# A decoder step on one core: transfers of the opening in a new order, four transposes in another bank, a copy and a store placed anew

## The chip, the cores and the metric

The kernel runs on one core of a Trainium2 chip. The metric is the time of one execution on the device in microseconds, lower is better. Engines are called by their names: TensorE (PE in the profile, its weight loads PEld), VectorE (DVE), ScalarE (ACT), GpSimd (POOL), SyncE (SP). DMAs are issued by an engine's sequencer (SPq, ACTq) and run beside the engines.

## The reference, cut to what matters

One layer of a decoder for 512 prompt tokens and 8 x 8 sample tokens, 576 in all, with model width 1024:

```
h   = x @ w_in                    # [u | v | q | k | v_attn | gate_A | gate_B]
A   = gelu(u) * spatial mix of LN(gelu(v)), in chunks of 128 positions
B   = sliding-window attention (window 128, 16 heads, 4 key heads), with a sink
      per head and a relative position bias: rel_bias[bucket(distance)]
m   = (sigmoid(gate_A) * (A @ w_pa) + sigmoid(gate_B) * (B @ w_pb)) @ w_o
x   = LN1(alpha * x + m)
x   = LN2(alpha * x + (silu(x @ w_gate) * (x @ w_up)) @ w_down)
```

Results are x for both groups, the new key and value windows, and the normalised v of the sample tokens.

## The kernel before, in words

**Numbers.** All is float32. Each operand of a large product is split in two: ScalarE casts it to the format `fp32r` (hi), VectorE subtracts that from the source (lo). `split` (lines 113 to 115) does this, so line 114 is always a cast on ScalarE and line 115 a subtraction on VectorE. A product is then three matmuls: hi by hi, hi by lo, lo by hi.

**Stages.** All weights lie in one array, `wall`, of units of 128 x 1024 (512 KB). SyncE fetches them in the order of use into three buffers (`fetch`, line 117); a unit is fetched when the split of an earlier one has freed its buffer. The stages are: the opening, which makes the first key tile and the first query tile; the other projections with the attention between them; the gMLP; merge; output projection; FFN; and the down projection with the last layer norm. From the opening on, TensorE goes from one stage into the next.

**The opening** (`projections_and_attention`, from line 715). Ten dummy products on zeros (`warm_up`, line 389) stand first. The 1024 input rows are cut in 8 chunks of 128. `load_x` (line 397) asks for the tokens of chunk k (`xT[:, k]`, 128 x 576) and for the first weight unit in pieces: weights 0:256 (chunk 0), tokens 0, weights 256:512, tokens 1, weights 512:1024, two small tables for the position bias (`bias_lookup`, line 418), tokens 2 and 3 in one transfer, weight unit 1, tokens 4 and 5, tokens 6 and 7, weight unit 2. Chunk k needs its tokens split and a 128 x 256 piece of weights split; it is then twelve matmuls of 288 columns into two tiles, `ps0_0` (keys) and `ps0_1` (queries): for each half of the tokens and each tile, hi by hi, hi by lo, lo by hi. After chunk 1 stands one product of the bias tables (`bias_products`, line 431), whose result VectorE copies into rows (lines 439, 440). `bias_tables` (line 442) writes these rows to DRAM 128 times (`circ`) and reads them back with a stride (`Bsel`); the first attention scores add them (line 574).

In this part a planner of the framework sets the order of each engine's instructions, by what it expects to be ready. Code under `manual_schedule()` (the pairs of merge and FFN, lines 998, 1099 and 1226) keeps the order in which it is written. `issue_after` holds what stands under it behind a given instruction of the same engine.

**After the opening.** The next tile (`psq`, the second query tile, from weight unit 2) starts on TensorE, then the value projection (`psav`, units 3 and 4). ScalarE and VectorE meanwhile empty the two tiles: `evac_k` (line 463) makes four casts of the keys on ScalarE (line 470), four subtractions on VectorE (line 475), and last a copy of the newest 192 key columns to `kraw` on ScalarE (line 478). `evac_q` (line 480) does the queries (lines 490 to 500). The second key tile, `psk`, is emptied in the same way later. A tile of PSUM is used again when all of its readers are done; there are three such tiles of two banks (`PS`, line 104) and two single banks (`bank`, line 107).

**The sample's attention.** `sample_scores` makes the weights S of the eight sample sequences. In the next PSUM pool, of eight single banks, `sample_turn` (line 675) transposes S in two groups of four (line 685), copies each out (line 686), and transposes the weights of the new tokens (line 688). The banks of the new pool lie where the old pool's tiles lay, so its first ones wait until the last gate tile, `psg`, has been copied out (line 815).

**The end.** `last_norm` (line 1337) normalises the last 128 rows in three pieces of columns: c0 (416) and c1 (416) by VectorE, c (192) by ScalarE and GpSimd. c0 is stored from ScalarE's queue, c1 from SyncE's (line 1353), c from SyncE's after c1 (line 1355).

Of the kernel before, what the change touches and what calls it, by code (L numbers as in the profile page):

```python
# [18 lines left out]
P = 128  # L19
D = 1024  # L20
KC = D // P
# [55 lines left out]
class Builder:  # L77
# [311 lines left out]
    def warm_up(self):  # L389

        z = self.C([512], mybir.dt.bfloat16, "zero")
        self.nc.vector.memset(z[:], 0.0)
        ps = self.bank("warm")
        for _ in range(10):
            self.mm(ps, z[:, :P], z[:], True, True)

    def load_x(self):
        nc, xT = self.nc, self.I["xT"]
        r = [self.C([2, NT], F32, f"xraw{i}") for i in range(4)]
        self.xraw = [r[k // 2][:, k % 2] for k in range(KC)]  # L400
        raw = self.praw.tile([P, 1024], F32, tag="raw", name="raw0")
        self.raws.append(raw)
        for c0, c1, k in ((0, 256, 0), (256, 512, 1), (512, 1024, None)):
            nc.sync.dma_start(out=raw[:, c0:c1], in_=self.I["wall"][0][:, c0:c1])
            if k is not None:
                nc.sync.dma_start(out=r[0][:, k], in_=xT[:, k])
        self.bias_lookup()
        nc.sync.dma_start(out=r[1][:], in_=xT[:, 2:4])
        self.fetch(1)
        nc.sync.dma_start(out=r[2][:], in_=xT[:, 4:6])  # L410
        nc.sync.dma_start(out=r[3][:], in_=xT[:, 6:8])
        self.fetch(2)

    def xact(self, k):
        return self.X[:, k, :NT], self.X[:, k, NT:]
# [23 lines left out]
        nc.vector.tensor_copy(out=self.rows, in_=o[:, :W].unsqueeze(1).to_broadcast([P, 4, W]))  # L439
        nc.vector.tensor_copy(out=self.rows_s, in_=o[:, W:NBIAS])  # L440

    def bias_tables(self):

        nc = self.nc
        cd = self.pd.tile([H, W, W], F32, name="circ")
        nc.sync.dma_start(
            out=cd.rearrange("h (m a r) i -> (h m) a r i", m=8, a=4),
            in_=self.rows.unsqueeze(1).to_broadcast([P, 4, 4, W]))
        self.Bsel = [self.C([8, P], F32, f"Bsel{i}") for i in range(2)]
        for i in range(2):  # L450
            src = bass.AP(cd.tensor, cd.offset + 8 * i * W * W, [[W - 1, P], [W * W, 8], [1, P]])
            nc.sync.dma_start(out=self.Bsel[i][:], in_=src)
# [10 lines left out]
    def evac_k(self, ps, c):  # L463
        nc = self.nc
        self.kt += [self.C([2, NT], F32R, f"kt{2 * c + i}") for i in range(2)]
        f = lambda a: a.rearrange("p (b c) -> p b c", b=2)
        for i in range(2):
            s = slice(64 * i, 64 * i + 64)
            for o in range(2):
                nc.scalar.copy(out=f(self.kt[2 * c + i][64 * o : 64 * o + 64, 0]), in_=ps[s, :, :HB])  # L470
        for i in range(2):
            t = self.kt[2 * c + i]
            s = slice(64 * i, 64 * i + 64)
            for o in range(2):
                nc.vector.tensor_tensor(
                    out=f(t[64 * o : 64 * o + 64, 1]), in0=ps[s, :, :HB], in1=f(t[s, 0]).bitcast(F32),
                    op=ALU.subtract)
        nc.scalar.copy(out=self.kraw[:, c, :], in_=ps[:, 1, HB - 192 : HB])  # L478

    def evac_q(self, ps, c):  # L480
        nc = self.nc
# [190 lines left out]
            out=S[:], in0=S[:], in1=rec.unsqueeze(2).to_broadcast([P, DB, SK]), op=ALU.mult)  # L672
        return S

    def sample_turn(self, S):
        nc = self.nc
        f32c = lambda s, n: self.C(s, F32, n)
        pnew = self.SG("pnew")
        nc.vector.tensor_copy(
            out=pnew[:, :NS].rearrange("p (b j) -> p b j", b=DB), in_=S[:, :, W:])  # L680
        pT = f32c([DB, P], "spT")
        for c in range(2):
            ps = self.bank(f"pst{c}")
            for b in range(4):
                nc.tensor.transpose(ps[:, P * b : P * b + P], S[:, 4 * c + b, :W], self.ident[:])
            self.turned = nc.scalar.copy(out=pT[:, 4 * c : 4 * c + 4].rearrange("p b q -> p (b q)"), in_=ps)
        ps2 = self.bank("pst2")
        nc.tensor.transpose(ps2[:NS, :P], pnew[:, :NS], self.ident[:])
        pN = f32c([DB, P], "spN")
        nc.vector.tensor_tensor(  # L690
            out=pN[:NS], in0=ps2[:NS, :P].unsqueeze(1).to_broadcast([NS, DB, P]),
            in1=self.bmask[:NS].unsqueeze(2).to_broadcast([NS, DB, P]), op=ALU.mult)
        return pT, pN
# [21 lines left out]
    def projections_and_attention(self):  # L715
        nc = self.nc
        self.X = self.px.tile([P, KC, 2 * NT], F32R, tag="x", name="X")
        self.XS = self.C([KC, P], F32R, "XS")
        misc = self.misc = self.C([1152], F32, "misc")
        self.kraw = misc[:, :384].rearrange("p (c t) -> p c t", c=2)  # L720
        self.Z = self.C([G, 4, 32], F32, "Z")
        self.kt, self.qs, self.u, self.T = [], {}, [], []
        self.warm_up()
        self.load_x()
        self.small_tables()
        tiles = [self.PS(f"ps0_{c}") for c in range(2)]
        for k in range(KC):
            if k % 4 == 0:
                u = self.unit(4, parts=4, ahead=0)
            for t0, t1 in ((0, HB), (HB, NT)) if k == 0 else ((0, NT),):  # L730
                self.split(self.X[:, k, t0:t1], self.X[:, k, NT + t0 : NT + t1], self.xraw[k][:, t0:t1])
            xh, xl = self.xact(k)
            for c in range(2):
                wh, wl = (w[:, k % 4, P * c : P * c + P] for w in u)
                for b in range(2):
                    s = slice(b * HB, (b + 1) * HB)
                    o = tiles[c][:, b, :HB]
                    self.mm(o, wh, xh[:, s], k == 0, False)
                    self.mm(o, wh, xl[:, s], False, False)
                    self.mm(o, wl, xh[:, s], False, k == KC - 1)  # L740
            if k == 1:
                self.bias_products()
        self.convert(2)
        self.bias_tables()
        self.convert(4)
        self.evac_k(tiles[0], 0)
        self.evac_q(tiles[1], 0)
        self.first_read = self.evacuated
        self.run(self.column_tile("q", 1))
        with self.tc.issue_after(self.placed.ins):  # L750
            nc.vector.tensor_copy(out=self.XS[:, :, :NS], in_=self.X[:, :, NP:NT].bitcast(F32))
            nc.vector.tensor_copy(out=self.XS[:, :, NS:], in_=self.X[:, :, NT + NP :].bitcast(F32))
        self.yB = []
        blocks = [(g, n) for g in range(G) for n in range(NB)]
        fills = FILLS
        probs = []
        self.values(lambda: probs.append(self.attention_scores(*blocks[len(probs)])))
        self.sample_bias()
        self.run(self.column_tile("q", 2))
        for i, (g, n) in enumerate(blocks):  # L760
            if n == 0:
                self.yB.append(self.C([2, NT], F32, f"yB{g}"))
            turned = self.attention_turn(g, n, probs[i])
            if i:
                with self.tc.issue_after(self.last_turned.ins):
                    self.attention_values(*waiting)
            if i + 2 < len(blocks):
                probs.append(self.attention_scores(*blocks[i + 2]))
                if i + 4 == len(blocks):
                    with self.tc.issue_after(self.selected.ins):  # L770
                        kc, vc = self.sample_keys()
            elif i + 1 < len(blocks):
                S = self.sample_scores(kc)
            if i:
                with self.tc.issue_after(self.lower.ins), self.tc.issue_after(self.shifted.ins):
                    self.run(fill)
            waiting = g, n, turned
            before_last = i + 2 == len(blocks)
            fill = self.column_tile(*fills[i], ahead=1 + before_last)
            next(fill, None)  # L780
            if i + 1 == len(blocks):
                with self.tc.issue_after(self.last_mm.ins):
                    self.attention_values(*waiting)
            next(fill, None)
            if i + 3 == len(blocks):
                self.run(fill)
        self.run(fill)
        self.sample = S, vc

    def sample_first(self):  # L790
        S, vc = self.sample
        turned = self.sample_turn(S)
        self.sample_rest = lambda: self.sample_values(vc, *turned)

    def run(self, gen):
# [541 lines left out]
    def last_norm(self, st, z, g, b, dst):  # L1337
# [12 lines left out]
        for k, queue in ((c0, nc.scalar), (c1, nc.sync)):  # L1350
            nc.vector.scalar_tensor_tensor(
                out=z[:, k], in0=z[:, k], scalar=r[:], in1=b[:, k], op0=ALU.mult, op1=ALU.add)
            sent = queue.dma_start(out=dst[:, k], in_=z[:, k])
        with self.tc.issue_after(sent.ins):
            nc.sync.dma_start(out=dst[:, c], in_=z[:, c])


def _weights(w_in, w_pa, w_pb, w_o, w_gate, w_up, w_down):
# [107 lines left out]
```

## Time and profile before

| what | us |
|---|---|
| runs shown, median (lowest to highest of 3) | 887.53 (887.2 to 889.0) |
| the profiled execution, its own time | 887.54 |
| its span, first to last instruction | 885.8 |
| TensorE busy in the span | 873.7 |
| VectorE / ScalarE / GpSimd busy | 630.7 / 405.8 / 195.5 |
| span from 0 to 12: TensorE busy | 9.52 |

Times in the profile are microseconds from the first instruction. A row of the timeline gives start, length, engine, line of the kernel, operation, tile written and tile read, shapes and count (rows that follow each other closely are merged), and in brackets how long the engine stood idle before it and what released it. `DMA` as a releaser is the landing of a transfer. A row of the table by stretches gives for each engine the busy time and in brackets the number of instructions, then the granted clock of TensorE as a share of full, the DMA engines' busy share, and GB/s moved. The chain of waits follows the work that ended last back from the end.

### The profile page before, as it was taken

The page shows a single profiled execution, that of the slowest core. Times are in us where ns is not written, and L with a number is a line of the kernel's source. Part 1 is how long each engine was busy: PE and PEld are TensorE (multiplying, and loading weights), DVE is VectorE, ACT ScalarE, POOL GpSimd, SP SyncE. Part 2 cuts the span into 40 slices and gives each one's busy share as a digit, 9 for nine tenths or more (in the row PEclk, how much of TensorE's full clock was granted, in tenths as well). Part 3 has the DMA queues.
Part 4 walks back from the last instruction along what each step waited for, and adds up shares of the span by engine and source line. Part 5 has one row for each costly group of instructions (what it writes and reads, how often), then busy time and mean ns, then how long its engine had stood idle before and what let it go on. Part 6 is the DMA issues. An engine that isn't in the chain of part 4 may idle for free.

```text
span 885.8 us, 14732 instructions
## 1 busy us (share of the span) xinstructions
PE 873.7 (99%) x5911; PEld 821.0 (93%) x5911; DVE 630.7 (71%) x934; ACT 405.8 (46%) x769; POOL 195.5 (22%) x205
## 2 busy tenths in 40 slices
PE   8999999999999999999999999999999999999996
PEld 7999999988899999999988999999999998888885
DVE  6778897646789789768777777777777789224237
ACT  6567566566355356334422544444444457111110
POOL 3013324242332113133302222222222210000003
PEclk9999999999999999999999999999999999999999
DMA  8431225144023224324450023233323325323202
GB/s 301 137 115 53 69 72 146 60 170 162 24 81 110 94 75 161 108 105 154 165 201 18 1 72 96 96 96 95 95 97 96 95 96 190 96 72 95 72 1 107
DMA packets 31168, 91.85 MB, mean 104 GB/s; under 512 B 3963, under 2 KB 9372, under 8 KB 31068
## 3 DMA queue, kind: packets, MB, share of 16 engines
q1 hardware_dynamic: 30908, 88.74, 30.6%
q10 hardware_dynamic: 192, 2.18, 0.6%
q8 instruction: 46, 0.75, 0.3%
q14 instruction: 22, 0.18, 0.1%
HBM read 86.77 MB, written 6.10 MB: 105 GB/s over the span
## 4 chain that ended last, share of the span: by engine, by line
PE 92%; DVE 4%; ACT 1%; issue 1%; DMA 1%; SPq 0%; POOL 0%; DVEq 0%; ACTq 0%; POOLq 0%
PE d L295 16%; PE xf L295 14%; PE zf L295 7%; PE acc_v L295 6%; PE acc_o L295 6%; PE pspa L295 6%; PE xg L295 5%; PE psu L295 5%; PE yf L295 4%; PE psq L295 3%; PE ffn L295 3%; PE zg L295 3%; PE xp L295 2%; PE psav L295 2%; PE psg L295 1%; PE yg L295 1%
## 5 line engine op out<-in xcount | busy, mean ns | idle before, releaser
L115 DVE TENSOR_TENSOR lo<-raw,hi 128x1024 fp32r<-128x1024 f32 (+1 forms) x78 | 89.8, 1159 | 96.7 <-ACT hi L114 96.3
L115 DVE TENSOR_TENSOR glo<-raw,ghi 128x1024 fp32r<-128x1024 f32 (+1 forms) x93 | 100.8, 1087 | 55.3 <-ACT ghi L114 55.3
L295 PE MATMUL d<-hi,h 128*128 128x512 f32 (+1 forms) x440 | 128.0, 368 | 0.0
L114 ACT CAST hi<-raw 128x1024 fp32r<-128x1024 f32 (+1 forms) x78 | 75.7, 984 | 105.9 <-PE d L295 82.6
L114 ACT CAST ghi<-raw 128x1024 fp32r<-128x1024 f32 (+1 forms) x93 | 83.4, 900 | 58.8 <-DVE raw L177 54.2
L295 PEld LDWEIGHTS d<-hi,h 128*128 128x128 f32 x440 | 79.8, 188 | 13.8
L295 PE MATMUL d<-lo,h 128*128 128x512 f32 (+1 forms) x242 | 89.6, 370 | 0.0
L177 POOL TENSOR_TENSOR raw<-raw,t 128x512 f32<-128x512 f32 x31 | 40.7, 1314 | 198.4 <-DVE glo L115 170.3
L177 POOL TENSOR_TENSOR t<-raw,raw 128x512 f32<-128x512 f32 x31 | 42.1, 1358 | 117.5 <-DVE raw L177 117.5
L295 PE MATMUL xf<-x1T,ghi 128*128 128x288 f32 x320 | 64.9, 295 | 0.0
L115 DVE TENSOR_TENSOR glo<-t,ghi 128x1024 fp32r<-128x1024 f32 x31 | 64.5, 2082 | 0.0
L295 PEld LDWEIGHTS d<-lo,h 128*128 128x128 f32 x242 | 45.6, 188 | 7.8
L295 PEld LDWEIGHTS xf<-x1T,ghi 128*128 128x128 f32 x320 | 51.3, 188 | 0.2 <-DVE u L226 0.2
L325 POOL TENSOR_SCALAR lnr<-lnmv 128x1 f32<-128x1 f32 (+1 forms) x15 | 12.3, 821 | 168.8 <-DVE lnmv L343 165.5
L608 POOL TENSOR_SCALAR_AFFINE_SELECT pc<-pt 128x512 fp32r<-128x512 f32 x24 | 23.1, 962 | 110.9 <-ACT pt L114 109.2
L295 PE MATMUL xf<-x1T,glo 128*128 128x288 f32 x160 | 47.1, 294 | 0.0
L295 PE MATMUL acc_o<-hi,m 128*128 128x512 f32 x144 | 46.4, 391 | 0.0
L295 PE MATMUL pspa<-yA,hi 128*128 128x288 f32 x256 | 44.6, 294 | 0.3 <-DVE yA L115 0.3
L295 PE MATMUL psu<-X,hi 128*128 128x288 f32 x256 | 44.1, 294 | 0.0
L584 ACT ACTIVATE work<-work,att 128x128 f32<-128x128 f32 x64 | 25.0, 392 | 40.9 <-DVE att L581 40.8
L295 PE MATMUL acc_v<-hi,X 128*128 128x512 f32 x128 | 41.6, 391 | 0.0
L295 PE MATMUL psq<-X,hi 128*128 128x288 f32 x224 | 38.8, 294 | 0.5 <-ACT misc L478 0.5
(367 smaller groups left out, 2476.3 us busy)
## 6 DMA issues: line engine op xcount, KB each, us to landing
raw<-in_wall_dram SPq DMA_DIRECT2D x133, 512.0 KB
xr<-in_xT_dram SPq DMA_DIRECT2D x8, 288.0 KB
z<-in_xtok_dram SPq DMA_DIRECT2D x4, 512.0 KB
xraw<-in_xT_dram SPq DMA_DIRECT2D x3, 576.0 KB
out_y_prompt_dram<-z SPq DMA_DIRECT2D x3, 512.0 KB
circ<-bout SPq DMA_DIRECT2D x1, 1024.0 KB
Bsel<-circ SPq DMA_DIRECT2D x2, 512.0 KB
kc<-in_kcT_dram SPq DMA_DIRECT2D x2, 512.0 KB
```

Of the source, the lines that this page charges most:

```text
L114: self.nc.scalar.copy(out=hi, in_=src)
L115: return self.nc.vector.tensor_tensor(out=lo, in0=src, in1=hi.bitcast(F32), op=ALU.subtract)
L177: sub = lambda e, out, x, y: e.tensor_tensor(out=out, in0=x, in1=y, op=ALU.subtract)
L295: self.last_mm = self.nc.tensor.matmul(out, l, r, start=start, stop=stop, **more)
L325: self.nc.gpsimd.tensor_scalar_add(r[:n], mv[:n, 1:2], EPS)
L584: nc.scalar.activation(out=pr[:, r], in_=sel[:, r], func=AF.Exp, bias=nm[:, r : r + 1], accum_out=rs[:, r : r + 1])
L608: self.selected = nc.gpsimd.affine_select(out=f(out[:, i]), in_=f(pt[:, i].bitcast(F32)), pattern=[[0, 4], [sign, P]], compare_op=cmp, fil ...
```

## The change

`warm_up` makes 6 dummy products, not 10. `load_x` asks for the transfers in this order: the first half of tokens 0 (288 columns), weights 0:256, the second half of tokens 0, weights 256:512, tokens 1, tokens 2, weights 512:1024, tokens 3, weight unit 1, tokens 4 and 5, tokens 6 and 7, the two bias tables, weight unit 2. It and the eight chunks stand under `manual_schedule()`, in the written order; a chunk now splits its own piece of weights (`opening_chunk`, new), behind its tokens, except that chunk 0 splits the second half of its tokens after its weights. `bias_products` moves from chunk 1 to the end of chunk 5. The write of the bias rows (`bias_rows`, cut out of `bias_tables`) follows `convert(2)`, under the same manual order. The copy to `kraw` in `evac_k` moves ahead of the subtractions. The first four transposes of S move into the old PSUM pool, into one of its two single banks. The last piece c is stored from ScalarE's queue, behind c0.

```diff
-        for _ in range(10):
+        for _ in range(6):
             self.mm(ps, z[:, :P], z[:], True, True)
...
-        for c0, c1, k in ((0, 256, 0), (256, 512, 1), (512, 1024, None)):
-            nc.sync.dma_start(out=raw[:, c0:c1], in_=self.I["wall"][0][:, c0:c1])
-            if k is not None:
-                nc.sync.dma_start(out=r[0][:, k], in_=xT[:, k])
-        self.bias_lookup()
-        nc.sync.dma_start(out=r[1][:], in_=xT[:, 2:4])
+        x = lambda k, s: nc.sync.dma_start(out=r[k // 2][:, k % 2, s], in_=xT[:, k, s])
+        w = lambda s: nc.sync.dma_start(out=raw[:, s], in_=self.I["wall"][0][:, s])
+        all_ = slice(0, NT)
+        x(0, slice(0, HB))
+        w(slice(0, 256))
+        x(0, slice(HB, NT))
+        w(slice(256, 512))
+        x(1, all_)
+        x(2, all_)
+        w(slice(512, 1024))
+        x(3, all_)
         self.fetch(1)
         nc.sync.dma_start(out=r[2][:], in_=xT[:, 4:6])
         nc.sync.dma_start(out=r[3][:], in_=xT[:, 6:8])
+        self.bias_lookup()
         self.fetch(2)
+
+    def opening_chunk(self, k, tiles):
+
+        if k % 4 == 0:
+            self.pieces.append((self.phi.tile([P, 1024], F32R, tag="hi", name=f"hi{k // 4}"),
+                                self.plo.tile([P, 1024], F32R, tag="lo", name=f"lo{k // 4}")))
+            self.unit_no += 1
+        w = slice(256 * (k % 4), 256 * (k % 4) + 256)
+        wh, wl = (t[:, w] for t in self.pieces[k // 4])
+        tokens = lambda t0, t1: self.split(
+            self.X[:, k, t0:t1], self.X[:, k, NT + t0 : NT + t1], self.xraw[k][:, t0:t1])
+        if k:
+            tokens(0, NT)
+        else:
+            tokens(0, HB)
+        self.split(wh, wl, self.raws[k // 4][:, w])
+        if k == 0:
+            tokens(HB, NT)
+        xh, xl = self.xact(k)
+        for b in range(2):
+            s = slice(b * HB, (b + 1) * HB)
+            for c in range(2):
+                o = tiles[c][:, b, :HB]
+                cols = slice(P * c, P * c + P)
+                self.mm(o, wh[:, cols], xh[:, s], k == 0, False)
+                self.mm(o, wh[:, cols], xl[:, s], False, False)
+                self.mm(o, wl[:, cols], xh[:, s], False, k == KC - 1)
+        if k == 5:
+            self.bias_products()
...
+        nc.scalar.copy(out=self.kraw[:, c, :], in_=ps[:, 1, HB - 192 : HB])
         for i in range(2):
             t = self.kt[2 * c + i]
...
-        nc.scalar.copy(out=self.kraw[:, c, :], in_=ps[:, 1, HB - 192 : HB])
...
+    def sample_half(self, S, c):
+        ps = self.bank(f"pst{c}")
+        for b in range(4):
+            self.nc.tensor.transpose(ps[:, P * b : P * b + P], S[:, 4 * c + b, :W], self.ident[:])
+        return ps
...
         self.warm_up()
-        self.load_x()
+        tiles = [self.PS(f"ps0_{c}") for c in range(2)]
+        with self.tc.manual_schedule():
+            self.load_x()
         self.small_tables()
...
+        with self.tc.manual_schedule():
+            for k in range(KC):
+                self.opening_chunk(k, tiles)
+            self.convert(2)
+            self.bias_rows()
         self.bias_tables()
...
-        self.sample = S, vc
+        self.sample = S, vc, self.sample_half(S, 0)
...
-        with self.tc.issue_after(sent.ins):
-            nc.sync.dma_start(out=dst[:, c], in_=z[:, c])
+            if k is c0:
+                with self.tc.issue_after(sent.ins):
+                    nc.scalar.dma_start(out=dst[:, c], in_=z[:, c])
```

More of the change, by code (lines that the diff above doesn't have):

```diff
@@ L440, in bias_products, with bias_rows @@
         nc.vector.tensor_copy(out=self.rows_s, in_=o[:, W:NBIAS])
-    def bias_tables(self):
+    def bias_rows(self):
         nc = self.nc
@@ L448, in bias_tables @@
             in_=self.rows.unsqueeze(1).to_broadcast([P, 4, 4, W]))
+        self.circ = cd
+    def bias_tables(self):
+        nc, cd = self.nc, self.circ
         self.Bsel = [self.C([8, P], F32, f"Bsel{i}") for i in range(2)]
@@ L673, in sample_scores, with sample_turn @@
         return S
-    def sample_turn(self, S):
+    def sample_half(self, S, c):
[3 more added lines that the diff above has]
+        return ps
+    def sample_turn(self, S, first):
         nc = self.nc
@@ L682, in sample_turn @@
         for c in range(2):
-            ps = self.bank(f"pst{c}")
-            for b in range(4):
-                nc.tensor.transpose(ps[:, P * b : P * b + P], S[:, 4 * c + b, :W], self.ident[:])
+            ps = self.sample_half(S, c) if c else first
             self.turned = nc.scalar.copy(out=pT[:, 4 * c : 4 * c + 4].rearrange("p b q -> p (b q)"), in_=ps)
@@ L723, in projections_and_attention @@
         self.warm_up()
-        self.load_x()
+        tiles = [self.PS(f"ps0_{c}") for c in range(2)]
+        with self.tc.manual_schedule():
+            self.load_x()
         self.small_tables()
[L726 to L743, printed above, removed]
+        with self.tc.manual_schedule():
[3 more added lines that the diff above has]
+            self.bias_rows()
         self.bias_tables()
@@ L787, in projections_and_attention @@
         self.run(fill)
-        self.sample = S, vc
+        self.sample = S, vc, self.sample_half(S, 0)
     def sample_first(self):
-        S, vc = self.sample
-        turned = self.sample_turn(S)
+        S, vc, first = self.sample
+        turned = self.sample_turn(S, first)
         self.sample_rest = lambda: self.sample_values(vc, *turned)
```

## The prediction

> **What bounds the kernel now.** I read first the head of the page and the table of busy time by stretches of the span.
>
> ```profile
> span 885.8 us, 14732 instructions
> ...
> PE 873.7 (99%) x5911; PEld 821.0 (93%) x5911; DVE 630.7 (71%) x934; ACT 405.8 (46%) x769; POOL 195.5 (22%) x205
> ```
> ```profile
> 4.00:7.00 3.00, 3.00 (x17) 1.99 (x14) 1.16 (x3) 1.74 (x4) 0.00 (x0) 1.00 0.86 251
> 7.00:10.00 3.00, 2.60 (x16) 1.97 (x14) 1.62 (x3) 0.71 (x2) 2.47 (x7) 1.00 0.97 356
> ...
> 80.00:90.00 10.00, 9.45 (x71) 9.07 (x70) 9.63 (x17) 6.79 (x19) 0.19 (x1) 1.00 0.25 79
> ...
> 180.00:190.00 10.00, 9.27 (x62) 8.50 (x62) 4.53 (x9) 4.61 (x8) 4.45 (x5) 1.00 0.21 53
> ...
> 870.00:885.80 15.80, 8.19 (x59) 7.58 (x57) 10.59 (x17) 0.46 (x1) 4.77 (x7) 0.89 0.25 100
> ```
>
> TensorE is idle for 12.1 us of 885.8: 7.6 after 870, 0.55 between 80 and 90, 0.73 between 180 and 190, and most of the rest in the opening. The change touches these four places, so it can win only what lies in those holes. The two in the middle are shown with their releasers below.
>
> The opening I read from the chain of waits (one fence) and from the timeline (the other).
>
> ```profile
> 4.07 5.95 DMA xraw<-in_xT_dram
> ...
> 21.44 6.32 PE psq L295 x48
> ```
> ```profile
> 2.98 0.40 ACT L114 CAST hi<-raw 128x256 fp32r<-128x256 f32 x1 [0.70 <-DMA raw<-in_wall_dram]
> ...
> 9.50 0.72 PE L295 MATMUL bias<-bsel 33*128 33x272 f32 x2
> ...
> 10.04 1.25 ACT L114 CAST X<-xraw 128x576 fp32r<-128x576 f32 x2 [2.09 <-DMA xraw<-in_xT_dram]
> ...
> 12.09 0.68 DVE L439 COPY bout<-bias 128x512 f32<-128x512 f32 x1
> ...
> 12.91 1.42 DVE L115 TENSOR_TENSOR lo<-raw,hi 128x256 fp32r<-128x256 f32 x4
> ...
> 14.17 1.25 ACT L114 CAST X<-xraw 128x576 fp32r<-128x576 f32 x2 [0.19 <-DMA xraw<-in_xT_dram]
> 14.24 2.76 DVE L115 TENSOR_TENSOR X<-xraw,X 128x576 fp32r<-128x576 f32 x4
> ...
> 21.28 0.69 PE L295 MATMUL psq<-X,hi 128*128 128x288 f32 x4
> ```
>
> A product takes 6.32/48 = 0.132 us, a chunk of twelve 1.58. The opening ends at 21.28, where the next tile starts. Before that the third and fourth chunks waited for tokens that landed at 10.04, and then VectorE, which runs 0.69 us per token split (2.76/4), 0.355 per weight split (1.42/4) and 0.82 for the two bias copies (12.09 to 12.91), was the late one.
>
> **The opening: transfers.** In KiB, from the shapes, 1,701 were asked for up to the tokens that landed at 10.04, and 3,365 up to the last ones, which landed at about 14.15: 406 per us. After the change 2,752 stand up to the pair of chunks 4 and 5, which is still one transfer. On the old line that is 10.04 + 1,051/406 = 12.6. Three microseconds around the issue of the small bias tables moved 251 GB/s where the next three moved 356; the tables now go behind all tokens, which gives back 105 x 3 / 356 = 0.9. So the pair lands at 11.75 (estimate; 12.6 if the dip stays, 11.4 if those microseconds reach the 406). Half tokens first let the first product start at about 4.2 (first landing before the cast at 2.98, some 0.7 for the next piece, a cast of 0.40). That start is worth nothing of itself: four chunks from 4.2, even with a stall or two, are done before 12.6, and chunk 4 waits for its pair anyway.
>
> From the landing: cast 0.73 with its handover, low tokens 0.78, low weights 0.36, so the third product of chunk 4 goes at 13.6; ten products 1.32; chunk 5 1.58. Chunk 5 ends at 11.75 + 4.78 = 16.53.
>
> **The opening: bias copies.** The chunks now stand in an order written by hand, and bias_products moves from chunk 1 to the end of chunk 5. Its two copies are VectorE instructions, emitted behind chunk 5's splits and ahead of chunk 6's. That such an order is kept shows where the pairs already have it:
>
> ```profile
> 533.46 0.45 ACT L1260 ACTIVATE g<-g 128x288 f32<-128x288 f32 x1 [2.44 <-DVE g L226]
> 533.81 1.03 ACT L114 CAST ghi<-raw 128x1024 fp32r<-128x1024 f32 x1
> ```
>
> ScalarE stood 2.44 us for the activation and did the cast emitted behind it only then. So VectorE will stand from about 14.8, when chunk 5 is split, until TensorE has done chunk 5 and the bias product. Queued behind are the splits of chunks 6 and 7, and TensorE waits for those. From the end of chunk 5: bias done 0.81 (start 0.09, busy 0.72), copies with handover 0.88, low tokens 0.75, low weights 0.36 and handover 0.06: the third product of chunk 6 goes 2.86 later, the chunk ends at 4.18, chunk 7 at 5.76. The opening ends at 16.53 + 5.76 = 22.29, later by 1.01 (0.66 to 1.86 with the landing). The stall that went, for tokens and splits, comes back as one for the bias copies.
>
> The other instructions that move with these steps are covered. The bias tables, on SP's queue now behind all tokens, land by about 14, and GpSimd's copy of one follows; the product that reads them goes at 16.6. The write of the bias rows stands on SP's queue behind the fetch that waits for chunk 7's last weight split, at 16.53 + 3.85 = 20.4, some 5.7 later than now, and the reads that follow it move as far.
>
> ```profile
> 21.29 1.01 SPq L452 DMA_DIRECT2D Bsel<-circ  x2
> ```
> ```profile
> 36.73 1.27 DVE L574 TENSOR_TENSOR work<-work,Bsel 128x512 f32<-128x512 f32 x2
> ```
>
> Between issue and first use lie 15.4 us, of which 10.7 are left (15.4 - 5.7 + 1.0), and the 5.95 of the token pair is the longest landing above. If that cover went, the first scores would wait.
>
> **The warm-up.** Six dummy products in place of ten free TensorE before the first data.
>
> ```profile
> 1.28 4.14 PE L295 MATMUL warm<-zero 128*128 128x512 bf16 x10 [1.28 <-DVE zero L392]
> ```
> ```profile
> 4.67 0.15 PEld L295 LDWEIGHTS <-zero 128*128 128x128 bf16 x1 [0.28 <-issue]
> ...
> 5.54 0.19 PEld L295 LDWEIGHTS ps<-X,lo 128*128 128x128 f32 x1
> ```
>
> Ten took 4.14, so 0.41 to 0.43 for 512 columns, half the later pace (0.132 for 288); full pace begins between 4.67 and 5.54, 3.4 to 4.3 us after the start. Six end at 3.84, a gap follows. If half pace lasts to about 8.5 it is hidden under the wait for the pair; I take nothing, with 0.6 as the bound (third rival). [...]
>
> **The key copy.**
>
> ```profile
> 81.69 0.40 ACT L584 ACTIVATE work<-work,att 128x128 f32<-128x128 f32 x1 [1.12 <-DVE att L581]
> ...
> 84.27 0.76 DVE L475 TENSOR_TENSOR kt<-psk,kt 64x576 fp32r<-64x576 f32 x1
> ...
> 85.07 0.32 ACT L478 COPY misc<-psk 128x192 f32<-128x192 f32 x1 [0.69 <-DVE kt L475]
> ...
> 85.44 0.80 PE L295 MATMUL psq<-X,hi 128*128 128x288 f32 x4 [0.55 <-ACT misc L478]
> ```
>
> The copy now comes before the four subtractions, into ScalarE's 1.12 us of idleness, which covers its 0.32. Next late is L475, done at 85.03, so TensorE starts at 85.08: 0.36 won (0 if the planner leaves it, 0.55 at most).
>
> **The sample's transposes.**
>
> ```profile
> 186.06 0.64 ACT L815 COPY g<-psg 128x576 f32<-128x576 f32 x1
> ...
> 186.76 1.09 PE L685 MATMUL pst<-ident,samS 128*128 128x128 f32 x8 [0.73 <-ACT g L815]
> 187.69 0.27 PE L688 MATMUL pst<-ident,pnew 128*64 128x128 f32 x1
> ```
>
> Eight take 0.93 (186.76 to 187.69). Four in a bank that is free run while g is copied: 0.46 of the 0.73. The other four still wait for L815. If the planner sets them among earlier products nothing is won: 0 to 0.46, and I take 0.46, since nothing but the last products is left then.
>
> **The last store.**
>
> ```profile
> 881.39 0.59 POOL L1349 TENSOR_TENSOR z<-z,ln 128x192 f32<-128x192 f32 x1 [0.57 <-ACT z L1348]
> 881.55 0.36 ACTq L1353 DMA_DIRECT2D out_y_prompt_dram<-z  x1
> 882.45 0.33 SPq L1353 DMA_DIRECT2D out_y_prompt_dram<-z  x1
> 882.88 0.38 SPq L1355 DMA_DIRECT2D out_y_prompt_dram<-z  x1
> ```
>
> The narrow piece is ready at 881.98 and ScalarE's queue free at 881.91, so it goes 0.9 earlier, and the last issue is 882.45 in place of 882.88. That is 0.43 at most and nothing if the wide piece landed last already; I take 0.35, near the issue gap.
>
> **The sum.** +1.01 - 0.36 - 0.46 - 0.35 = -0.16. The profiled execution took 887.54 (span 885.8 and 1.74 around it; the median of the runs shown is 887.53): 887.4. Its own range, over the landing and the bounds above, is 886.9 to 889.0.
>
> **Rivals.** First, the bias copies do not hold VectorE (the planner moves them although the order is by hand, so the change does not do what it says). Then 0.6 for the bias product and 3.17 for two chunks follow 16.53: 20.30, a gain of 0.98, in all -2.15: 885.4 (885.0 at the early landing). For it: before, the planner did put these copies 2 us after their product. Against it: the wait at 533.46.
>
> Second, slower: the weights of the value projection. Their second tile is fetched at the same 20.4 (before: 14.36), and its cast may stand ahead of the key evacuation on ScalarE.
>
> ```profile
> 14.36 0.33 SPq L124 DMA_DIRECT2D raw<-in_wall_dram x1
> ```
> ```profile
> 18.82 1.05 ACT L114 CAST hi<-raw 128x1024 fp32r<-128x1024 f32 x1 [1.00 <-DMA raw<-in_wall_dram]
> 20.68 2.57 ACT L470 CAST kt<-ps 64x576 fp32r<-64x576 f32 x4 [0.81 <-PE ps L295]
> ...
> 29.54 1.54 DVE L495 SCALAR_TENSOR_TENSOR qs<-psq,qs 64x576 fp32r<-64x576 f32 x2 [1.20 <-ACT Z L493]
> ```
> ```profile
> 33.51 1.92 PE sc L295 x16
> ```
>
> From L470 to the end of L495 the chain has 31.08 - 20.68 - 1.20 = 9.2. A landing 4.4 after the issue (as at 18.82) puts the cast's end at 25.85 and the scores at 35.05, where TensorE arrives at 33.51 + 1.01 = 34.5: 0.55 lost. At the 5.95 of the token pair it is 2.1: 889.5. The kernel is slower from a landing 4.1 after the issue, and by over 0.2% from 5.8. Against it: the planner may well run the key casts first, and then this costs nothing.
>
> Third, half pace until 11.7, two spells of work rather than one: 31 of the 72 products of chunks 0 to 5 at 0.24, 41 at 0.132: chunk 5 ends at 17.1, 0.6 later: 888.0.
>
> **How the numbers follow.** Forecast 0.52, first rival 0.28, second 0.11, third 0.09. A measurement of this kernel tells 0.2%, 1.8 us, from no change. Faster by more: three quarters of the first rival and a tenth of the forecast, 0.26. Slower: nearly all of the second and a little of forecast and third, 0.13. Within: 0.61. The range reaches from the first rival's 885.0 to the forecast's upper end, 889.0.
>
> **What would show it.** Right: VectorE idle from about 15 to 17.5 with the bias copies next, TensorE idle some 2 us inside chunk 6, the next tile starting near 22.3; the waits for L478 and L815 shrunk to 0.2 and 0.3; last issue near 882.3. Wrong: chunk 6 following chunk 5 without that hole; the pair of chunks 4 and 5 landing before 10.7, where the opening breaks even; a new wait at the first scores; dummies' pace beyond chunk 1.

## The result, and the profile after

| | before | after |
|---|---|---|
| median of the timed runs | 887.38 us (16 runs, 886.24 to 889.52) | 889.76 us (16 runs, 888.28 to 890.57) |
| ratio, 95% interval | 1 | 1.0024 (1.0017 to 1.0032) |
| profiled execution | 887.54, span 885.8 | 889.52, span 887.8 |

The kernel became slower by 0.24%, 2.1 us (0.0024 x 887.38; the medians lie 2.4 apart). The forecast was 887.4, no change that can be measured; the time lies beyond the range's upper end of 889.0. What came is the second rival, on top of the forecast's opening.

The head of the page after, and its table of what TensorE waited for (us in total, times, the longest):

```profile
span 887.8 us, 14731 instructions
...
PE 874.9 (99%) x5907; PEld 821.4 (93%) x5907; DVE 630.8 (71%) x934; ACT 405.4 (46%) x769; POOL 192.6 (22%) x205
```
```profile
PE psq L295 <- DVE lo L115: 1.0, 1, 1.0
PE ps L295 <- ACT hi L114: 0.9, 2, 0.6
PE ps L295 <- DVE X L115: 0.8, 1, 0.8
PE pst L717 <- ACT g L847: 0.3, 1, 0.3
PE psq L295 <- DVE kt L515: 0.3, 1, 0.3
```

The busy share of TensorE is 99% as before: it says nothing here. The waits do. The first and the third row name VectorE and are the two holes. The first is new; before, the third was two waits of at most 0.4. The second row is two waits for a weight cast in the opening (0.62 at 7.24, 0.26 at 13.18). The last two rows are the shrunk waits of the sample's transposes and of the key copy. Where the holes lie is read from the table by stretches (the columns are the stretch, its length, and busy us of PE, PEld, DVE, ACT, POOL, then the granted clock, the DMA share and GB/s); first after, then the same stretches of before where the prediction doesn't show them:

```profile
4.00:7.00 3.00, 2.61 (x13) 2.25 (x12) 0.91 (x4) 1.23 (x3) 0.00 (x0) 1.00 0.96 277
...
10.00:14.00 4.00, 3.66 (x24) 3.00 (x22) 2.23 (x5) 2.32 (x7) 0.14 (x1) 1.00 1.03 410
14.00:20.00 6.00, 5.20 (x32) 4.28 (x32) 3.16 (x7) 3.67 (x7) 1.26 (x3) 1.00 0.28 101
20.00:40.00 20.00, 18.83 (x143) 18.14 (x144) 14.22 (x23) 10.40 (x19) 0.00 (x0) 1.00 0.69 218
```
```profile
10.00:14.00 4.00, 3.19 (x21) 2.74 (x21) 3.26 (x8) 3.82 (x8) 0.01 (x1) 1.00 1.03 407
14.00:20.00 6.00, 5.97 (x45) 5.74 (x44) 5.37 (x8) 4.40 (x5) 3.92 (x2) 1.00 0.95 325
20.00:40.00 20.00, 20.00 (x162) 20.00 (x162) 14.25 (x24) 9.81 (x19) 0.00 (x0) 1.00 0.55 172
```

From 10 to 14 us the new order wins 0.47 (3.66 busy us in place of 3.19). From 14 to 20 TensorE loses 0.77 (5.97 - 5.20), and between 20 and 40, where before it never stood, it loses 1.17 (20.00 - 18.83).

**The first hole.** VectorE's and TensorE's rows of the timeline after, and one of before:

```profile
14.54 0.51 DVE L115 TENSOR_TENSOR lo<-raw,hi 128x256 fp32r<-128x256 f32 x1
17.89 0.69 DVE L474 COPY bout<-bias 128x512 f32<-128x512 f32 x1 [2.84 <-PE bias L295]
...
18.71 0.75 DVE L115 TENSOR_TENSOR X<-xraw,X 128x576 fp32r<-128x576 f32 x1
```
```profile
17.13 0.72 PE L295 MATMUL bias<-bsel 33*128 33x272 f32 x2
...
18.02 0.69 PE L295 MATMUL psq<-X,hi 128*128 128x288 f32 x4
19.51 0.40 PE L295 MATMUL ps<-X,hi 128*128 128x288 f32 x1 [0.80 <-DVE X L115]
...
22.87 0.43 PE L295 MATMUL psq<-X,lo 128*128 128x288 f32 x2
```
```profile
21.81 0.43 PE L295 MATMUL psq<-X,lo 128*128 128x288 f32 x2
```

VectorE stood 2.84 us for the bias product, with the splits of chunks 6 and 7 queued behind its copies, and TensorE then stood for the split of chunk 6. The planner put the first four products of the next tile into the hole (18.02), so the tile's start can't be compared; its fifth product can: 22.87 against 21.81, later by 1.06.

**The second hole.** The fetch of the value projection's second weight unit on SyncE's queue, then ScalarE, VectorE and TensorE after, and TensorE before:

```profile
20.82 0.33 SPq L124 DMA_DIRECT2D raw<-in_wall_dram  x1
```
```profile
25.75 1.05 ACT L114 CAST hi<-raw 128x1024 fp32r<-128x1024 f32 x1 [8.08 <-DMA raw<-in_wall_dram]
26.82 2.58 ACT L509 CAST kt<-ps 64x576 fp32r<-64x576 f32 x4
29.41 0.32 ACT L510 COPY misc<-ps 128x192 f32<-128x192 f32 x1
```
```profile
29.76 3.06 DVE L515 TENSOR_TENSOR kt<-ps,kt 64x576 fp32r<-64x576 f32 x4 [1.70 <-ACT misc L510]
32.85 1.54 DVE L534 SCALAR_TENSOR_TENSOR qs<-ps,qs 64x576 fp32r<-64x576 f32 x2
...
37.51 1.22 DVE L115 TENSOR_TENSOR lo<-raw,hi 128x1024 fp32r<-128x1024 f32 x1
```
```profile
34.41 2.83 PE L295 MATMUL sc<-kt,qs 128*128 128x256 f32 x16
...
38.79 0.53 PE L295 MATMUL psq<-X,lo 128*128 128x288 f32 x2 [1.02 <-DVE lo L115]
...
39.29 0.34 PE L295 MATMUL psav<-hi,X 128*128 128x256 f32 x1
```
```profile
33.35 2.08 PE L295 MATMUL sc<-kt,qs 128*128 128x256 f32 x16
...
36.20 0.28 PE L295 MATMUL psav<-hi,X 128*128 128x256 f32 x1
```

ScalarE stood 8.08 us for that unit, whose cast is queued ahead of the key casts L509. The keys were ready in the accumulator by 22.87; their casts began at 26.82, where before they began at 20.68. The subtractions, the queries (L534) and a weight split stand behind them on VectorE. TensorE feels it twice: the sixteen score products take 2.83 instead of 2.08 (0.75), and the products of the query tile behind them wait 1.02 for the split at 37.51. The scores began 1.06 late (34.41 - 33.35); the products of the values behind them resume 3.09 late (39.29 - 36.20). So the second hole costs 2.03: 0.75 at the scores and 1.28 behind them.

**The small parts**, after:

```profile
88.31 0.77 PE L295 MATMUL psq<-X,hi 128*128 128x288 f32 x4 [0.29 <-DVE kt L515]
```
```profile
188.67 0.60 PE L717 MATMUL pst<-ident,samS 128*128 128x128 f32 x4
...
189.56 0.66 PE L717 MATMUL pst<-ident,samS 128*128 128x128 f32 x4 [0.29 <-ACT g L847]
```
```profile
880.20 0.28 PE L295 MATMUL d<-hi,h 128*128 128x256 f32 x1
...
884.74 0.33 SPq L1385 DMA_DIRECT2D out_y_prompt_dram<-z  x1
```

The wait before the query tile is 0.29 in place of 0.55, the one in the transposes 0.29 in place of 0.73. The last product of after starts 7.6 before the end of its span, that of before (at 877.91) 7.89: 0.29 won. Together +1.06 + 2.03 - 0.26 - 0.44 - 0.29 = +2.10, against 2.0 between the spans.

### The profile page after: what moved, and what is told of

The parts are those of the page before. It is cut to its first block, busy times and chain, and to the rows that moved or that the text cites. A ratio compares the mean times of both kernels' runs of the same rounds, so it can differ in the third digit from the quotient of the medians.

```text
span 887.8 us, 14731 instructions
## 1 busy us (share of the span) xinstructions
PE 874.9 (99%) x5907; PEld 821.4 (93%) x5907; DVE 630.8 (71%) x934; ACT 405.4 (46%) x769; POOL 192.6 (22%) x205
## 4 chain that ended last, share of the span: by engine, by line
PE 90%; DVE 5%; ACT 2%; DMA 1%; issue 1%; SPq 0%; POOL 0%; DVEq 0%; ACTq 0%; POOLq 0%
PE d L295 16%; PE xf L295 14%; PE zf L295 7%; PE acc_v L295 6%; PE acc_o L295 6%; PE pspa L295 6%; PE xg L295 5%; PE psu L295 5%; PE yf L295 4%; PE ffn L295 3%; PE psq L295 3%; PE zg L295 3%; PE xp L295 2%; PE psg L295 1%; PE yg L295 1%
```

## The experiments

The theory after the result: the bias copies hold VectorE (+1.06); the late fetch, with its cast ahead of the key casts, holds the scores (+2.03); the three small parts win 1.0 and are independent. The rivals: that either hole comes from something else in the opening (the transfers' order, the warm-up, the pair's landing), or that the small parts do not win what their waits show. The kernel before, timed beside them again, took 887.65 us in the first four, 887.54 in the next four and 887.42 in the last.

**1. The bias copies behind all splits** (against the kernel after). The bias product stays at the end of chunk 5; only the two VectorE copies, now in a function bias_copies, move.

```
+        self.bias_o = o
+
+    def bias_copies(self):
+
+        nc, o = self.nc, self.bias_o
...
                 self.opening_chunk(k, tiles)
             self.convert(2)
+            self.bias_copies()
             self.bias_rows()
```

> The changed kernel, with VectorE's two bias copies moved behind all splits of the opening; the bias product stays behind chunk 5. Theory: the copies hold VectorE, so the opening ends late (+1.06) and the fetch of the value weights is issued late (20.82), which costs another 2.0 up to 39 us. Both go: VectorE never waits for the bias product, the next tile runs on from about 20.9 (before 21.28, changed 22.87 with four products done earlier), the fetch is issued at about 17, the waits at the scores and behind them vanish, and the time is 886.3, about 1.1 below the kernel before. Rival: the loss comes with the new order of the transfers and the six dummies, whatever the copies do: then the time stays near 889.7.

Measured: 886.64 us, ratio 0.9989 (0.9981 to 0.9998), so 3.1 us below the kernel after by the ratios (1.0024 - 0.9989 = 0.0035). VectorE, SyncE's queue, ScalarE and TensorE of its trace:

```profile
18.21 0.68 DVE L479 COPY bout<-bias 128x512 f32<-128x512 f32 x1
```
```profile
17.18 0.33 SPq L124 DMA_DIRECT2D raw<-in_wall_dram  x1
```
```profile
21.54 1.05 ACT L114 CAST hi<-raw 128x1024 fp32r<-128x1024 f32 x1 [3.78 <-DMA raw<-in_wall_dram]
22.62 2.57 ACT L514 CAST kt<-ps 64x576 fp32r<-64x576 f32 x4
```
```profile
21.15 0.69 PE L295 MATMUL psq<-X,hi 128*128 128x288 f32 x4
...
36.07 0.28 PE L295 MATMUL psav<-hi,X 128*128 128x256 f32 x1
```

The 2.84 us wait is gone, the opening ends at 21.15, and the values resume at 36.07: both 0.13 ahead of before. So one moved pair of instructions closes both holes. The second hangs on the first: with VectorE free, chunk 7's weights are split earlier (by 17.15), their buffer comes free, the fetch goes at 17.18 instead of 20.82 and lands at about 21.5. The cast still stands ahead of the key casts, but these now start at 22.62, early enough.

**2. The key casts ahead of the unit's cast** (against the kernel after); the bias copies hold VectorE as they do there. The name kcopied is the key copy's instruction.

```
-        nc.scalar.copy(out=self.kraw[:, c, :], in_=ps[:, 1, HB - 192 : HB])
+        self.kcopied = nc.scalar.copy(out=self.kraw[:, c, :], in_=ps[:, 1, HB - 192 : HB])
...
-        self.convert(4)
+        self.convert(3)
         self.evac_k(tiles[0], 0)
+        with self.tc.issue_after(self.kcopied.ins):
+            self.convert(4)
```

> The changed kernel, with the cast of the value projection's second weight unit held behind the key evacuation on ScalarE; bias copies as in the changed kernel. Theory: the opening still ends late (22.87), but the key casts start at about 22.8 in place of 26.82, the scores find their operands, the 2.0 lost up to 39 us goes: 0.1 to 0.4 above the kernel before, 887.7. Rival: the late landing (25.70) itself is the trouble, not its place on ScalarE: then the value projection waits for the unit at about 30 and the time stays 1 to 2 above the kernel before.

Measured: 887.81 us, 1.0004 (0.9995 to 1.0013).

```profile
23.07 2.58 ACT L509 CAST kt<-ps 64x576 fp32r<-64x576 f32 x4 [5.00 <-PE ps L295]
...
26.07 1.05 ACT L114 CAST hi<-raw 128x1024 fp32r<-128x1024 f32 x1
```
```profile
23.27 0.42 PE L295 MATMUL psq<-X,lo 128*128 128x288 f32 x2
...
34.82 2.08 PE L295 MATMUL sc<-kt,qs 128*128 128x256 f32 x16
...
37.67 0.28 PE L295 MATMUL psav<-hi,X 128*128 128x256 f32 x1
```

The first hole stays (23.27, 1.46 late in this execution), the second is gone: the scores take 2.08 again, and the values resume 1.47 late, 0.01 more than the opening left them. In time it is worth 0.0020, 1.8 us, of the 2.03.

**3. The fetch not held** (against the kernel after): weight unit 1 in a buffer of its own, so that the fetch of the unit in question needn't wait for chunk 7's split. The order on ScalarE is untouched.

```
-            raw = self.praw.tile([P, 1024], F32, tag="raw", name=f"raw{i}")
+            if i == 1:
+                raw = self.C([1024], F32, "raw1")
+            else:
+                raw = self.praw.tile([P, 1024], F32, tag="raw", name=f"raw{i}")
```

> The changed kernel, with weight unit 1 in a buffer of its own, so that the fetch of the value projection's second unit needs no buffer that chunk 7 frees; bias copies as in the changed kernel. Theory: that fetch is issued some 1.6 us earlier or more (it stands behind one small transfer that needs the bias copies), its cast ends by 24.4 and not at 26.80, the scores find their operands at 34.4, nearly all of the 2.0 goes: 0.1 to 0.6 above the kernel before. Rival: the fetch's time is not what counts, the time stays near 2 above.

Measured: 887.81 us, 1.0006 (0.9998 to 1.0015), the same as experiment 2.

```profile
18.34 1.05 ACT L114 CAST hi<-raw 128x1024 fp32r<-128x1024 f32 x1 [0.29 <-DMA raw<-in_wall_dram]
22.87 2.58 ACT L512 CAST kt<-ps 64x576 fp32r<-64x576 f32 x4 [3.48 <-PE ps L298]
```

Here the fetch goes at 12.39. Its cast keeps its place ahead of the key casts and costs nothing, since it is done 3.48 us before the keys. Experiments 2 and 3 take away one each of two conditions, the queue order and the late landing, and either removes the second hole. Both must hold for it.

**4. The three small parts alone** (on the kernel before): the key copy, the sample's transposes and the last store as in the change, the opening untouched.

> The kernel before with the three small parts only: key copy ahead of the subtractions, four transposes in the old pool, last piece on ScalarE's queue; the opening is as before. Theory: their sum is what the traces show, 0.26 + 0.44 + 0.29, so about 1.0 below the kernel before, 886.4; the wait before psq shrinks from 0.55 to 0.2 or 0.3, that before pst from 0.73 to 0.3. Rival: the key copy ahead of the subtractions holds VectorE by 0.35 in the first key evacuation and gives part of it back there: 0.3 to 0.6 below.

Measured: 886.26 us, 0.9989 (0.9980 to 0.9998), a gain of 1.0 (0.2 to 1.8); predicted were 0.36 + 0.46 + 0.35 = 1.17. The waits in its trace are 0.28 at the query tile and 0.29 in the transposes, as after.

**5. The opening alone** (on the kernel before): all of the change but those three.

> The kernel before with the opening of the change alone (order of the transfers, half tokens, six dummies, bias product at the end of chunk 5 in an order by hand), without the key copy, the sample's transposes and the last store. Theory: the opening costs 1.06 by the held VectorE and 2.03 by the late fetch, 3.1 in all, and the three small parts, measured alone at a ratio of 0.9989, are independent of it: ratio 1.0030 to 1.0038, 890.1 to 890.8. Rival: the key copy that now stands ahead of the subtractions made the late keys later, so that without it the opening costs 0.3 less: ratio about 1.0030 or less.

Measured: 890.41 us, 1.0034 (1.0021 to 1.0046). With experiment 4's 0.9989 this makes 1.0023, and the whole measured 1.0024: within their intervals, of about 0.001 each way, the parts add. The trace has one thing that the times can't separate:

```profile
38.80 0.34 PE L295 MATMUL psav<-hi,X 128*128 128x256 f32 x1
```

The values resume at 38.80, 0.49 earlier than after. In the kernel after, the key copy of the opening stands ahead of the subtractions, and these start only behind it (29.41 to 29.76, 0.35); the rest of the 0.49 comes from the unit's cast, which began 0.16 earlier here (25.59 against 25.75). So by the traces the key copy's move gave back in the opening about what it won at 88 us.

**6. The key copy behind the subtractions again** (on experiment 1).

```
-        nc.scalar.copy(out=self.kraw[:, c, :], in_=ps[:, 1, HB - 192 : HB])
...
+        nc.scalar.copy(out=self.kraw[:, c, :], in_=ps[:, 1, HB - 192 : HB])
```

> The kernel with the bias copies behind all splits, with the key copy put back behind the four subtractions. Theory: the stall ahead of the query tile at about 85 us grows from 0.29 back to 0.55, 0.26 us lost; the 0.35 us for which the first subtraction stood behind the copy in the opening goes, and is worth nothing because the scores are not late there: 886.9. Rival: the subtractions' hold counts, and the time falls instead: 886.3.

Measured: 886.95 us, 0.9991 (0.9982 to 1.0000), 0.3 above experiment 1; the wait before the query tile is back:

```profile
PE psq L295 <- ACT misc L522: 0.5, 1, 0.5
```

With the keys in time, the 0.35 in the opening is hidden and the move is worth its 0.26. Medians 0.3 apart, of runs that spread over 0.7 and 1.3, don't show this by themselves; the wait does.

**7. Ten dummy products** (on experiment 1).

```
-        for _ in range(6):
+        for _ in range(10):
```

> The kernel with the bias copies behind all splits, with ten dummy products instead of six ahead of the first data. Theory as in the prediction: the first products starting early is worth nothing, since chunk 4 waits for its pair anyway; four more dummies push the first product from 3.89 to about 5.4 us, and the time stays at 886.6, give or take 0.3. Rival: four chunks from 5.4 no longer fit before the pair is split at about 13.0, and the start is lost in part: 0.5 to 1.5 us slower. Rival of the clock: six dummies leave TensorE at half pace longer, so that ten make it faster: 886.0 or less.

Measured: 886.43 us, 0.9985 (0.9977 to 0.9994), within 0.2 of experiment 1.

```profile
5.16 1.04 PE L295 MATMUL ps<-X,hi 128*128 128x288 f32 x2
...
21.36 0.69 PE L295 MATMUL psq<-X,hi 128*128 128x288 f32 x4
```

The first product starts at 5.16 in place of 3.90, and the opening ends at 21.36 in place of 21.15. The early start is worth nothing that can be measured. That holds for the half token transfer too as far as it serves this start; no run takes that transfer out alone.

**8. Tokens of chunks 4 to 7 one chunk at a time** (on experiment 1), since TensorE still waits in the opening for the pair of chunks 4 and 5.

```
-        nc.sync.dma_start(out=r[2][:], in_=xT[:, 4:6])
-        nc.sync.dma_start(out=r[3][:], in_=xT[:, 6:8])
+        x(4, all_)
+        x(5, all_)
+        x(6, all_)
+        x(7, all_)
```

> The kernel with the bias copies behind all splits, and the tokens of chunks 4, 5, 6 and 7 as four transfers of one chunk instead of two transfers of two. Theory: with the bias copies out of the way, the next thing that TensorE waits for in the opening is the pair of chunks 4 and 5, which landed at about 12.2 us; half of it holds 288 KiB, 0.7 us at the 406 KiB per us of the kernel before. So chunk 4 should start 0.5 to 0.7 us earlier, and the median go from 886.64 to about 886.0. Rival: the splits on VectorE (0.69 to 0.76 us for tokens, 0.36 to 0.42 for weights, eight chunks) or the four extra issues on the queue are late next, and nothing is won: 886.6.

Measured: 885.83 us, 0.9982 (0.9973 to 0.9990), faster than both kernels. The next tile starts at

```profile
20.71 0.69 PE L295 MATMUL psq<-X,hi 128*128 128x288 f32 x4
```

0.44 before experiment 1.

**9. The second weight unit in halves as well** (on experiment 8): its first half ahead of chunk 4's tokens, its second behind chunk 5's.

> The kernel with the bias copies behind all splits and the tokens of chunks 4 to 7 as four transfers, with the second weight unit fetched in two halves: the first (chunks 4 and 5) ahead of the tokens of chunk 4, the second behind those of chunk 5. Theory: the tokens of chunk 4 then stand behind 256 KiB less, so land 0.63 us earlier (256 at 406 KiB per us), and the hole of about 0.4 us that TensorE still has at the start of chunk 4 (13.32 to 13.71 us in the kernel with the tokens split) closes; median 885.83 less 0.2 to 0.4: 885.4 to 885.6. Rival: VectorE, which splits a chunk in 1.1 us, or the weights of chunk 6, which now land later, are late next: 885.8 or more.

Measured: 885.58 us, 0.9981 (0.9972 to 0.9991), the fastest here: 1.8 below the kernel before and, by the ratios (1.0024 - 0.9981), 3.8 below the kernel after. The opening ends earlier again:

```profile
20.12 0.69 PE L295 MATMUL psq<-X,hi 128*128 128x288 f32 x4
```

The trace gives 0.59 where the medians give 0.25; experiments 8 and 9 are not told apart by their times.

## Why the prediction was wrong, point by point

- **The pair's landing**: 11.75 with bounds of 11.4 and 12.6. Chunk 4's cast began at 12.15, inside the bounds and 0.4 later than taken. The dip to 251 GB/s, counted as won back, was partly still there: 277 from 4 to 7 us. Chunk 5 ended at about 17.1, not 16.53.
- **The bias copies hold VectorE**: right. +1.01 predicted, +1.06 measured, but as a sum of two misses: chunk 5 ended 0.6 later, and the hole behind it was that much cheaper because the planner filled 0.53 us of it with four products of the next tile. That the two cancel is luck.
- **The second rival**: this is the step that failed. The forecast took nothing for the late weight unit, with "the planner may well run the key casts first, and then this costs nothing" and a chance of 0.11. That sentence had a row against it that the prediction itself quotes: before, ScalarE ran this unit's cast at 18.82 and the key casts behind it at 20.68. The order was there already; only the fetch had been early. Written-order stalls were believed for VectorE in one paragraph and doubted for ScalarE in another without a row that told the two apart.
- **Its size**: by its own working a landing 4.88 after the issue (20.82 to 25.70) costs 0.55 + 0.48 = 1.03; it cost 2.03. The rival's chain ends at the scores, and there the loss was smaller, 0.75, though the fetch went 0.42 later than 20.4 and the subtractions stood 0.35 for the key copy (a wait that the paragraph on the key copy placed only at 85 us). The other 1.28 were lost behind the scores, 1.02 of them in the wait for the weight split that VectorE ran behind the queries, which the rival didn't follow. So it is luck that the 889.5 which it gives for a landing after 5.95 lies near the measured time.
- **The first rival**, copies that don't hold VectorE, would have been 885.4. Experiment 1 makes that kernel: 886.64. Its opening ended at 21.15 where the rival had 20.30, most of it because chunk 5 ended 0.6 later.
- **The third rival**, half pace until 11.7, did not come. In experiment 1 and in the kernel after, products run at the full pace from about 6 us (two took 0.57 to 0.85 up to 5.5, and 0.43 from 6.3). That is 4 to 5 us after the first dummy (1.27), where the prediction read 3.4 to 4.3 from the trace of before; between the six dummies (to 4.01) and the first product (3.89 and 3.90) there was next to no gap. That half pace would last for two spells of work was an estimate; neither trace shows it.
- **The small parts**: -0.36, -0.46 and -0.35 predicted, -0.26, -0.44 and -0.29 measured.

With the second rival's 2.03 put into the sum the forecast would have been 887.4 + 2.0 = 889.4, in place of the measured 889.76 (profiled 889.52). So of the terms of the sum one was taken at nothing, and the rest came within 0.1 each, the largest of them by luck.

Left open: what sets the time from the issue of this fetch to its cast, 4.46 us before (14.36 to 18.82), 4.36 in experiment 1 (17.18 to 21.54), 4.93 after (20.82 to 25.75) and 5.95 in experiment 3 (12.39 to 18.34). In the kernel after, 16 GB/s moved from 20 to 21 us, 45 from 21 to 22, and 217 only from 22 on. No run here takes that apart.

## What to carry to other kernels

Before a copy of a TensorE result is written into the program of an engine that keeps its order (here VectorE stood 2.84 us for the bias product and ScalarE 8.08 us for the weight unit), count what is queued behind it: the two short copies cost 3.1 us, a third of it directly and two thirds because the split that they held up also released the buffer of a fetch. For every fetch that a change delays, look up in the profile of before which instruction on the casting engine already stands behind its cast, and price the wait as if that order stayed. The new order of the opening was worth nothing against the old one even with the hold gone (0.9989 with it in experiment 1, 0.9989 without it in experiment 4); it won, by some 0.07% (0.9982 in experiment 8, with intervals that overlap), only when the transfers that TensorE waits for were made as small as their use.

## What else the runs showed

- Before, single runs of one kernel spread over 3.2 us (886.10 to 889.26, 35 runs) and with the copies late over 0.7 (886.36 to 887.03, 11 runs). Part of the former is TensorE's clock. In the profiled execution of experiment 4, whose opening is that of before, the next tile began at 22.78 instead of 21.28, and the granted clock (third number from the end) was half for three microseconds:

```profile
12.00:15.00 3.00, 3.00 (x13) 3.00 (x14) 3.00 (x8) 2.69 (x7) 0.00 (x0) 0.50 1.00 391
```

Of these 1.5 us a late landing gave 0.37 (the first product behind it went at 11.14 instead of 10.77); the other 1.1 are the half clock. The runs fit: of 76 runs of the kernel before beside the experiments (a 77th took 2220.41 us), the 13 that took 888.49 or more all have a mean granted clock of 0.995 or 0.996, and the 63 that took 888.23 or less all have 0.997 to 0.999. Three microseconds at half clock lower that mean by 0.0017 (estimate: 0.5 x 3 / 886). What halves the clock is open: ahead of it TensorE had stood 1.9 us for a token cast, but in experiment 3 it stood 1.6 us for a weight cast, and the products behind it came 0.13 us apart from 9.0 to 13.4 us, the full pace. So one profiled opening is only one draw, here 1.5 us wide.

- A read of an accumulator by ScalarE and one by VectorE stood one behind the other: the first subtraction waited for the 0.32 us copy of the same tile (29.41 to 29.76), though both only read it. In experiment 6, where the copy stands behind, it started at 25.57, as the last of the four key casts ended, though it uses the first two alone. Whether the chip or the waits that the program sets make this so, no run here tells.
